# Attention scores of a hybrid decoder step: the two float parts of a query stacked on 128 partitions

## The chip, the cores and the metric

The kernel is one program on one core of a Trainium2 chip. The metric is the device time of one execution in microseconds (us). TensorE is called PE in the rows (its weight loads PEld), VectorE DVE, ScalarE ACT, GpSimd POOL and SyncE SP.

## What is computed

One inference step of one decoder layer, in float32, for 1024 prompt tokens and 64 sample tokens (8 requests of 8) that share the weights:

```python
# per group of tokens
q, k, v, mq, mk, mv, og, ig, lf = project_mixers(rmsnorm(y, g_mix), w_in, ...)   # 1024 -> 2312 columns
att = swa(q, k, v, sinks)            # 8 query heads, 2 key heads of 64; a window of 128 keys
h   = mlstm(mq, mk, mv, ig, lf)      # 4 heads, a matrix memory
y  += concat(att, headnorm(h) * sigmoid(og)) @ w_out
y  += cross_attend(rmsnorm(y), memory keys and values)   # 4 heads of 64, 256 memory tokens
y  += (silu(xn @ w_gate) * (xn @ w_up)) @ w_down         # xn = rmsnorm(y), hidden 2816
out = rmsnorm(y)
```

In the prompt, a block of 128 queries reads its own and the previous block of keys, so one head's scores for one block are a 128 x 256 tile with a contraction over 64. In the cross-attention the scores of one head for one block are 128 x 256 with a contraction over 64 as well. The caches, the states and the memory keys and values are outputs too.

## The kernel before, in words

**Exact float32 by parts.** Every large product is made from fp32r operands. `split` (L101 to L109) rounds an array into a high part on ACT (L102) and puts the remainder, the low part, on DVE (L103, or POOL for some weights). A product is then three matmuls: high x high, high x low, low x high (`mm3`). All matmuls stand under the helper's line L85, so the rows are told apart by their tiles: `mm` is the PSUM tile of the projections, `sc` of the scores, `pt` of transposes, `o` of the attention outputs.

**Order of the stages.** The projections and the mLSTM come first (to about 298 us of the span; the mLSTM's gates use POOL, and its blocks keep `mvx`, `CS` and `QZ` in the slots of tag "c"). Then comes the windowed attention: 16 calls of `swa_unit`, one for a block of 128 queries and a pair of query heads per key head; between the calls a generator, `fill`, hands out projections (the output gate and a part of the output projection) in the numbers of the list `nfill`. Then the output projection of the attention heads and the cross-attention, chunk by chunk of tokens, with eight calls of `cross_unit` between them, and last the FFN, with the final norm and the stores. Engines take their instructions in a fixed order each. A scheduler orders them while the program is built, by the order of the text and by its own estimate of when operands and buffers are ready; so matmuls of different tiles stand interleaved on PE.

**Scores in `swa_unit`.** The query is split into `qhl` (two times 128 columns for the high parts, the same for the low). The two key heads lie on partitions 0 to 63 and 64 to 127, in the keys `khi` and `klo` as in the queries. For each of two query heads the loop runs over the three products and, innermost, over the two key heads: 12 matmuls of 64 rows and 256 columns, whose neighbours use different halves of the rows and write different PSUM banks. DVE then adds the mask and takes the maximum (L703), ACT the exponential (L622), DVE the scaling (L627), PE transposes (L717), ACT copies (L718), and four float32 matmuls on half the columns make the output `o`, which ACT copies into the place of the query (L724).

**Scores in `cross_unit`.** The same with two heads of a feature tile: `qhl` from the projected query `xq`, the memory keys in `kvhl`, 12 matmuls of 64 rows per call, then the maximum (L866, L884), the exponential (L887) and the scaling (L891).

**Buffers.** The slots of tag "c" are nine: in the windowed attention the keys `khi` and `klo`, the values `vp`, the memory's `kvf`, the sample's `VC` and a rotation of `pp`. PSUM has two banks for `sc`, three for `mm`, two for `pt` and one for `o`. Temporary tiles have ten buffers.

Of the kernel before, what the change touches and what calls it, by code (L numbers as in the profile page):

```python
# [9 lines left out]
F32 = mybir.dt.float32  # L10
F32R = mybir.dt.float32r
AF = mybir.ActivationFunctionType
# [3 lines left out]
P = 128  # L16
D = 1024
NK = D // P                 # feature tiles of the model width
TP = 1024                   # prompt tokens
TS = 64                     # sample tokens (8 requests x 8)  # L20
T = TP + TS
NB = TP // P                # prompt token blocks
CH = [(0, 384), (384, 768), (768, 1088)]
CHE = [(0, 416), (416, 832), (832, 1088)]   # where the last one ends the kernel
FT = 22                     # feature tiles of the FFN
# [4 lines left out]
# columns of the vectors packed by the host  # L30
# [3 lines left out]
# columns of the constants  # L34
C_ID, C_ONE, C_CAUS, C_CAUSS, C_BM, C_M0, C_M1 = 0, 128, 256, 384, 448, 456, 712
C_N = 968
# columns of the constants for the gates
# [5 lines left out]
def tile_hymba_step(  # L43
# [79 lines left out]
    def load_ahead(srcs):  # L123
        """The weights in the order of their use, each loaded one step ahead of it."""
        todo, ahead = iter(srcs), []

        def step():
            for src, eng in todo:
                ahead.append(load_w(src, 8, eng=eng))
                break  # L130

        def next_w():
            step()
            return ahead.pop(0)

        step()
        return next_w
# [19 lines left out]
    # ================= stage 1: x, split; sums of squares =================  # L157
# [22 lines left out]
    # the first two tiles run along with the arrival of x  # L180
# [24 lines left out]
    # token-major rstd  # L205
# [150 lines left out]
    # rows (block, head) of prompt; rows (head) of sample  # L356
# [40 lines left out]
    # the weight of the state before the block, as rows  # L397
# [33 lines left out]
    # the upper half of the partitions holds the odd heads  # L431
# [20 lines left out]
    # M4: mq pair 0, mq pair 1, mk pair 0, mk pair 1; later the head outputs  # L452
# [4 lines left out]
    # the heads' norm weights with the half of sigmoid(x) = (1 + tanh(x / 2)) / 2  # L457
# [5 lines left out]
    def mlstm_ps():  # L463
        """PSUM for num | den of the heads: the row tiles of odd and even heads go to different banks."""
        b = [ptps([2, 129]), ptps([2, 129])]
        return b, [b[h % 2][:, h // 2] for h in range(4)]

    def mlstm_w(src, m):
        """The weight of the state, by head pair, on the partitions of the heads."""
        wb = tmp([2, m], name="wb")  # L470
        for h2 in range(2):
            nc.sync.dma_start(wb[h2 * 64:h2 * 64 + 64],
                              src.rearrange("o (j z t) -> o z j t", z=2, t=m)[:, h2].to_broadcast([64, 2, m]))
        return wb

    def mlstm_head_out(nb, blk, m, c0, junk):
        """num | den of the heads in PSUM -> normalised heads, transposed into M4."""
        rec = small(4, "rec", 2)
        for z in range(2):
            V.tensor_copy(rec[:m, z::2], nb[z][:m, :, P])  # L480
        V.scalar_tensor_tensor(rec[:m], rec[:m], -1.0, rec[:m], ALU.mult, ALU.max)
        V.tensor_tensor(rec[:m], rec[:m], emt[:m, blk * 4:blk * 4 + 4], ALU.max)
        V.reciprocal(rec[:m], rec[:m])
        hh = tmp([4, P], name="hh")
        for z in range(2):
            V.tensor_tensor(hh[:m, z::2], nb[z][:m, :, 0:P],
                            rec[:m, z::2].unsqueeze(2).to_broadcast([m, 2, P]), ALU.mult)
        q2 = small(4, "q2", 2)
        for h in range(4):
            A.activation(junk[:m], hh[:m, h, :], AF.Square, accum_out=q2[:m, h:h + 1])  # L490
        done = rstd_from(q2[:m], q2[:m], P)
        V.tensor_tensor(hh[:m], hh[:m], q2[:m].unsqueeze(2).to_broadcast([m, 4, P]), ALU.mult)
        ht = ops([4, P])
        for h in range(4):
            TE.transpose(ht[:, h, :m], hh[:m, h, :], ident[:m, :m])
        for h in range(4):
            A.activation(M4[h][:, c0:c0 + m], ht[:, h, :m], AF.Copy, scale=hg[:, h:h + 1])
        return done

    def mlstm_S(blk, m, c0, bc, caus):  # L500
        """S^T[s, t] of the four heads, weighted."""
        dd = bc
        G.tensor_tensor(dd[:m], caus.unsqueeze(1).to_broadcast([m, 4, m]), bc[:m], ALU.subtract)
        for h in range(4):
            A.activation(dd[:m, h, :], dd[:m, h, :], AF.Exp, bias=gg[:m, blk * 4 + h:blk * 4 + h + 1])
        kq = [scps(), scps()]
        for h in range(4):
            pr = slice((h % 2) * 64, (h % 2) * 64 + 64)
            mm(kq[h % 2][:m, (h // 2) * m:(h // 2) * m + m], M4[2 + h // 2][pr, c0:c0 + m], M4[h // 2][pr, c0:c0 + m])
        S = tmp([4, m], name="S")  # L510
        for h2 in range(2):
            V.tensor_tensor(S[:m, h2::2], kq[h2][:m, 0:2 * m].rearrange("p (j t) -> p j t", j=2),
                            dd[:m, h2::2], ALU.mult)
        return S
# [102 lines left out]
    def softmax_pieces(pieces, mx, nbias, es=None):  # L617
        """P = exp(0.125 s + bias) / (sum + es) in place for the (row, piece) scores."""
        n = len(pieces)
        l = small(4, "l", 2)  # L620
        for i, a in enumerate(pieces):
            A.activation(a, a, AF.Exp, scale=0.125, bias=nbias[:, i:i + 1], accum_out=l[:, i:i + 1])  # L622
        if es is not None:
            V.tensor_tensor(l[:, 0:n], l[:, 0:n], es, ALU.add)
        V.reciprocal(l[:, 0:n], l[:, 0:n])
        for i, a in enumerate(pieces):
            V.tensor_scalar_mul(a, a, l[:, i:i + 1])  # L627
# [56 lines left out]
    def swa_unit(blk, jp):  # L684
        k0 = max(0, (blk - 1) * P)
        mask = c[:, C_M0:C_M0 + 256] if blk == 0 else c[:, C_M1:C_M1 + 256]
        qhl = tmp([2, 2, P], F32R, name="qhl")
        qh, ql = qhl[:, 0], qhl[:, 1]
        for j2 in range(2):
            split(qh[:, j2, :], ql[:, j2, :], qc[2 * jp + j2][:, blk * P:blk * P + P])  # L690
        sc = [scps(), scps()]
        for j2 in range(2):
            cs = slice(j2 * 256, j2 * 256 + 256)
            for z, (a, b_) in enumerate(((qh, khi), (qh, klo), (ql, khi))):
                for kv in range(2):
                    pr = slice(kv * 64, kv * 64 + 64)
                    mm(sc[kv][:, cs], a[pr, j2, :], b_[pr, k0:k0 + 256], z == 0, z == 2)
# [50 lines left out]
    class Next:  # L748
        """Operands of the GEMM behind a norm: (y * g) split; rstd goes on its output."""
# [68 lines left out]
    for u in range(2 * NB):  # L818
        if u == 0:
            swa_sample()  # L820
        swa_unit(u // 2, u % 2)
        for _ in range(nfill[u]):
            next(fill, None)
# [4 lines left out]
    kvhl = slot("c", [4, 256], F32R, name="kvhl")  # L828
    kvh, kvl = kvhl[:, 0:2], kvhl[:, 2:4]
    split(kvh, kvl, kvf[:, 0:2])  # L830
# [5 lines left out]
    # weights of this stage in the order of their use  # L836
# [31 lines left out]
    def cross_unit(pair, f):  # L868
        """Two blocks of prompt tokens, one pair of heads."""
        bs = slice(pair * 256, pair * 256 + 256)  # L870
        qhl = tmp([2, 256], F32R, name="qhl")
        split(qhl[:, 0], qhl[:, 1], xq[f][:, bs])
        sc = [scps(), scps()]
        for i in range(2):
            ts = slice(i * P, i * P + P)
            for z, (a, b_) in enumerate(((0, kvh), (0, kvl), (1, kvh))):
                for h2 in range(2):
                    pr = slice(h2 * 64, h2 * 64 + 64)
                    mm(sc[h2][:, i * 256:i * 256 + 256], qhl[pr, a, ts], b_[pr, f, :], z == 0, z == 2)
# [168 lines left out]
def _consts():  # L1048
# [19 lines left out]
    # sample window: rows (request of the pair, kv, group, token)  # L1068
# [13 lines left out]
def _tiles(w, cols=None):  # L1082
    """[K, F] -> [F/128, 128, K/128, 128]"""
# [5 lines left out]
def _pack(i):  # L1089
# [23 lines left out]
    for base, g in ((V_MIX, a["g_mix"][0]), (V_CROSS, a["g_cross"][0]), (V_FFN, a["g_ffn"][0]),  # L1113
# [5 lines left out]
    s = a["attn_sinks"][0].reshape(2, 2, 2)          # kv, pair, j2  # L1119
# [10 lines left out]
                         a["state_mlstm_n"][0][..., None]], -1)          # b h d 129  # L1130
    r["st_C"] = np.ascontiguousarray(
        st.reshape(4, 2, 4, 64, 129).transpose(1, 3, 0, 2, 4).reshape(P, 4, 4, 129))
    ck = a["cache_mem_k"][0].reshape(8, 256, 2, P)                       # b m f (h2 d)
# [42 lines left out]
```

## Time and profile before

| what | value |
|---|---|
| three runs | 1380.97, 1387.66, 1389.80 us; median 1387.66 |
| profiled execution | span 1380.3 us (first to last instruction; no time of its own is given beside the span) |
| PE, PEld, DVE, ACT, POOL busy | 1343.5, 1266.2, 622.2, 444.6, 190.3 us |
| matmuls | 8352 records, of them 192 scores of the windowed attention and 96 of the cross-attention |
| granted clock of PE | 0.995 of full on average |

A busy share says little by itself: matmuls are pipelined, so that a record of 0.33 us can follow its predecessor after 0.17 us. What one matmul costs is read from the distance between the starts of neighbours. The stages are told apart by time: windowed attention about 298 to 425 us, output projection and cross-attention to about 592 us, FFN from there to the end.

### The profile page before, as it was taken

How to read it: one execution, taken by the hardware profiler on the slowest of the kernel's cores; microseconds unless marked ns; L12 is line 12 of the kernel's file. 1: busy time of each engine (PE TensorE's matmuls, PEld its weight loads, DVE VectorE, ACT ScalarE, POOL GpSimd, SP SyncE). 2: the span in 40 equal slices, each digit the busy share in tenths (PEclk: the TensorE clock that was granted, in tenths of full speed). 3: DMA queues.
4: the chain of work that ended last, by engine and by line, in shares of the span. 5: the costliest groups of instructions: out<-in, count | busy, mean ns of one | idle time of the engine just before them, and what ended most of it. 6: DMA issues, size and time to landing. Idle time of an engine off the chain costs nothing.

```text
span 1380.3 us, 20544 instructions
## 1 busy us (share of the span) xinstructions
PE 1343.5 (97%) x8352; PEld 1266.2 (92%) x8352; DVE 622.2 (45%) x1373; ACT 444.6 (32%) x1024; POOL 190.3 (14%) x167
## 2 busy tenths in 40 slices
PE   7999999999999898999999999999999999999997
PEld 6999988887888786799999999999999999999997
DVE  7224345467766778835323332332233232423245
ACT  4322332447754666721221011201121121112133
POOL 3000110100003551110111011101110011001123
PEclk9999999999999999999999999999999999999999
DMA  5122413110311224102111111111112120111113
GB/s 228 40 74 62 146 56 121 38 47 16 131 46 57 97 92 163 52 16 62 47 31 62 46 47 31 51 42 46 47 32 61 31 62 31 62 32 50 43 37 124
DMA packets 38807, 88.26 MB, mean 64 GB/s; under 512 B 6593, under 2 KB 14209, under 8 KB 38713
## 3 DMA queue, kind: packets, MB, share of 16 engines
q1 hardware_dynamic: 38713, 86.95, 19.6%
q8 instruction: 66, 1.08, 0.3%
q14 instruction: 28, 0.23, 0.1%
HBM read 79.54 MB, written 7.38 MB: 63 GB/s over the span
## 4 chain that ended last, share of the span: by engine, by line
PE 58%; DVE 3%; ACT 1%; issue 0%; DMA 0%; POOL 0%; DVEq 0%; ACTq 0%; POOLq 0%
PE mm L85 57%; DVE nlo L109 1%; PE o L85 0%; DVE y L955 0%; PE pt L85 0%; DVE nb L866 0%; DVE wlo L103 0%; DMA ck<-cm_k 0%; PE sc L85 0%; ACT sp L887 0%; ACT sq L773 0%; DVE qhl L103 0%; DVE ss L777 0%; DVE yo L1043 0%; PE pt L897 0%
## 5 line engine op out<-in xcount | busy, mean ns | idle before, releaser
L85 PE MATMUL mm<-nhi,wlo 128*128 128x384 f32 (+1 forms) x1056 | 344.4, 326 | 0.0
L85 PE MATMUL mm<-nlo,whi 128*128 128x384 f32 (+1 forms) x1056 | 344.1, 326 | 0.0
L85 PE MATMUL mm<-nhi,whi 128*128 128x384 f32 (+1 forms) x1056 | 344.0, 326 | 0.0
L102 ACT ACTIVATE whi<-wraw 128x1024 fp32r<-128x1024 f32 (+1 forms) x105 | 109.4, 1042 | 345.9 <-PE mm L85 295.1
L85 PEld LDWEIGHTS mm<-nhi,whi 128*128 128x128 f32 x1056 | 198.2, 188 | 0.1
L85 PEld LDWEIGHTS mm<-nhi,wlo 128*128 128x128 f32 x1056 | 198.2, 188 | 0.1
L85 PEld LDWEIGHTS mm<-nlo,whi 128*128 128x128 f32 x1056 | 198.2, 188 | 0.0
L1005 POOL TENSOR_TENSOR gate<-gate,rstd 128x384 f32<-128x384 f32 (+1 forms) x66 | 78.3, 1187 | 656.3 <-ACT gate L1004 656.3
L85 PE MATMUL mm<-hlo,whi 128*128 128x384 f32 (+3 forms) x480 | 157.1, 327 | 0.0
L85 PE MATMUL mm<-hhi,whi 128*128 128x384 f32 (+3 forms) x480 | 156.9, 327 | 0.0
L85 PE MATMUL mm<-hhi,wlo 128*128 128x384 f32 (+3 forms) x480 | 156.9, 327 | 0.0
L103 DVE TENSOR_TENSOR wlo<-wraw,whi 128x1024 fp32r<-128x1024 f32 (+1 forms) x93 | 112.1, 1205 | 45.6 <-ACT whi L102 41.9
L1008 DVE TENSOR_TENSOR h<-mm,gate 128x384 f32<-128x384 f32 (+1 forms) x66 | 35.4, 536 | 193.9 <-PE mm L85 189.0
L1018 DVE TENSOR_TENSOR y<-y,mm 128x384 f32<-128x384 f32 (+1 forms) x120 | 63.6, 531 | 118.6 <-PE mm L85 118.6
L85 PE MATMUL mm<-xhi,whi 128*128 128x384 f32 (+1 forms) x288 | 98.6, 342 | 0.0
L85 PE MATMUL mm<-xlo,whi 128*128 128x384 f32 (+1 forms) x288 | 98.1, 341 | 0.0
L85 PE MATMUL mm<-xhi,wlo 128*128 128x384 f32 (+1 forms) x288 | 97.3, 338 | 0.0
L1002 DVE TENSOR_TENSOR gate<-mm,rstd 128x384 f32<-128x384 f32 (+1 forms) x66 | 35.4, 536 | 123.5 <-PE mm L85 123.5
L85 PEld LDWEIGHTS mm<-hlo,whi 128*128 128x128 f32 x480 | 90.1, 188 | 0.4 <-issue 0.3
L85 PEld LDWEIGHTS mm<-hhi,whi 128*128 128x128 f32 x480 | 90.2, 188 | 0.2 <-issue 0.2
L85 PEld LDWEIGHTS mm<-hhi,wlo 128*128 128x128 f32 x480 | 90.2, 188 | 0.2 <-issue 0.2
L102 ACT ACTIVATE hhi<-h 128x384 fp32r<-128x384 f32 (+1 forms) x66 | 33.2, 503 | 158.7 <-DVE h L1008 158.6
(343 smaller groups left out, 2169.6 us busy)
## 6 DMA issues: line engine op xcount, KB each, us to landing
wraw<-wg SPq DMA_DIRECT2D x22, 512.0 KB
wraw<-wu SPq DMA_DIRECT2D x22, 512.0 KB
wraw<-wd SPq DMA_DIRECT2D x40, 256.0 KB
wraw<-wout SPq DMA_DIRECT2D x32, 256.0 KB
wraw<-win_f SPq DMA_DIRECT2D x13, 512.0 KB
xraw<-xT SPq DMA_DIRECT2D x8, 544.0 KB
y<-xT SPq DMA_DIRECT2D x8, 544.0 KB
o_y<-yo SPq DMA_DIRECT2D x16, 208.0 KB
```

Source lines behind the costliest of these rows:

```text
L85: return TE.matmul(out, lhsT, rhs, start=start, stop=stop)
L102: A.activation(hi, src, AF.Copy)
L103: (eng or V).tensor_tensor(lo, src, hi.bitcast(F32), ALU.subtract)
L109: V.scalar_tensor_tensor(lo, src, scale, hi.bitcast(F32), ALU.mult, ALU.subtract)
L1002: V.tensor_tensor(t, ga, fr[:, c0:c1], ALU.mult)
L1005: G.tensor_tensor(t, t, fr[:, c0:c1], ALU.mult)
L1008: V.tensor_tensor(h, ua, t, ALU.mult)
L1018: V.tensor_tensor(y[d][:, c0:c1], y[d][:, c0:c1], acc, ALU.add)
```

## The change: what it does

- The keys of the windowed attention are copied into four new tiles `kst` of the slots "c": for each key head and each part (high, low), the 64 rows stand on both halves of the partitions. POOL makes these eight copies of 64 x 1088.
- A new helper `stack` makes a tile `qst` of a query: for each of the two heads in it, the high part on that head's own half of the partitions and the low part on the other half. That is two ACT and two DVE instructions of 64 x 256 for 256 queries.
- A score is then two matmuls over all 128 rows: (high, low) against the high keys on both halves, and (high, low) against the low keys. The product low x low, left out before, comes in. There are 8 matmuls for a unit instead of 12, and the two key heads come one after the other.
- The units are taken in another order: both blocks of a pair of blocks for one pair of heads, and then the other pair of heads, so that one `stack` serves two units.
- In the cross-attention `kvhl` becomes two tiles `kvs` with the keys of each head on both halves (two splits of 64 x 512 and four POOL copies of 64 x 512), and `cross_unit` uses `stack` and 8 matmuls.

```diff
-    def swa_unit(blk, jp):
+    kst = []
+    for kv in range(2):
+        pr = slice(kv * 64, kv * 64 + 64)
+        both = []
+        for src in (khi, klo):
+            t = slot("c", [T], F32R, name="kst")
+            for z in range(2):
+                G.tensor_copy(t[z * 64:z * 64 + 64], src[pr].bitcast(F32))
+            both.append(t)
+        kst.append(both)
+    def stack(src):
+        st = tmp([2, 256], F32R, name="qst")
+        for z in range(2):
+            p_, q_ = slice(z * 64, z * 64 + 64), slice((1 - z) * 64, (1 - z) * 64 + 64)
+            A.activation(st[p_, z], src[p_], AF.Copy)
+            V.tensor_tensor(st[q_, z], src[p_], st[p_, z].bitcast(F32), ALU.subtract)
+        return st
+    qst = [None, None]
+    def swa_unit(bp, jp, bi):
+        blk = 2 * bp + bi
+        if bi == 0:
+            for j2 in range(2):
+                qst[j2] = stack(qc[2 * jp + j2][:, bp * 256:bp * 256 + 256])
         k0 = max(0, (blk - 1) * P)
         mask = c[:, C_M0:C_M0 + 256] if blk == 0 else c[:, C_M1:C_M1 + 256]
-        qhl = tmp([2, 2, P], F32R, name="qhl")
-        qh, ql = qhl[:, 0], qhl[:, 1]
-        for j2 in range(2):
-            split(qh[:, j2, :], ql[:, j2, :], qc[2 * jp + j2][:, blk * P:blk * P + P])
         sc = [scps(), scps()]
-        for j2 in range(2):
-            cs = slice(j2 * 256, j2 * 256 + 256)
-            for z, (a, b_) in enumerate(((qh, khi), (qh, klo), (ql, khi))):
-                for kv in range(2):
-                    pr = slice(kv * 64, kv * 64 + 64)
-                    mm(sc[kv][:, cs], a[pr, j2, :], b_[pr, k0:k0 + 256], z == 0, z == 2)
+        for kv in range(2):
+            for j2 in range(2):
+                cs = slice(j2 * 256, j2 * 256 + 256)
+                for z in range(2):
+                    mm(sc[kv][:, cs], qst[j2][:, kv, bi * P:bi * P + P], kst[kv][z][:, k0:k0 + 256],
+                       z == 0, z == 1)
 ...
-        swa_unit(u // 2, u % 2)
+        swa_unit(u // 4, u // 2 % 2, u % 2)
 ...
-    kvhl = slot("c", [4, 256], F32R, name="kvhl")
-    kvh, kvl = kvhl[:, 0:2], kvhl[:, 2:4]
-    split(kvh, kvl, kvf[:, 0:2])
+    kvs = [slot("c", [2, 2, 256], F32R, name="kvs") for _ in range(2)]
+    for h2 in range(2):
+        pr, po = slice(h2 * 64, h2 * 64 + 64), slice((1 - h2) * 64, (1 - h2) * 64 + 64)
+        split(kvs[0][pr, h2], kvs[1][pr, h2], kvf[pr, 0:2])
+        for z in range(2):
+            G.tensor_copy(kvs[z][po, h2], kvs[z][pr, h2].bitcast(F32))
 ...
     def cross_unit(pair, f):
-        """Two blocks of prompt tokens, one pair of heads."""
         bs = slice(pair * 256, pair * 256 + 256)
-        qhl = tmp([2, 256], F32R, name="qhl")
-        split(qhl[:, 0], qhl[:, 1], xq[f][:, bs])
+        st = stack(xq[f][:, bs])
         sc = [scps(), scps()]
-        for i in range(2):
-            ts = slice(i * P, i * P + P)
-            for z, (a, b_) in enumerate(((0, kvh), (0, kvl), (1, kvh))):
-                for h2 in range(2):
-                    pr = slice(h2 * 64, h2 * 64 + 64)
-                    mm(sc[h2][:, i * 256:i * 256 + 256], qhl[pr, a, ts], b_[pr, f, :], z == 0, z == 2)
+        for h2 in range(2):
+            for i in range(2):
+                for z in range(2):
+                    mm(sc[h2][:, i * 256:i * 256 + 256], st[:, h2, i * P:i * P + P], kvs[z][:, h2, f, :],
+                       z == 0, z == 1)
```

The rest of the diff removes comments.

## Rows read from the trace of the kernel before

**Rows 1.** The page's head and part 1: busy us (share) and instructions by engine.

```profile
span 1380.3 us, 20544 instructions
...
PE 1343.5 (97%) x8352; PEld 1266.2 (92%) x8352; DVE 622.2 (45%) x1373; ACT 444.6 (32%) x1024; POOL 190.3 (14%) x167
```

**Rows 2.** Stretches: length; PE, PEld, DVE, ACT, POOL busy us (instructions); clock; DMA.

```profile
298.00:355.00 57.00, 56.83 (x377) 43.32 (x376) 38.16 (x177) 38.02 (x136) 0.00 (x0) 0.94 0.06 20
355.00:425.00 70.00, 67.56 (x465) 56.87 (x464) 50.51 (x174) 43.55 (x137) 2.50 (x1) 1.00 0.28 95
465.00:535.00 70.00, 64.20 (x433) 55.11 (x434) 53.96 (x110) 45.42 (x112) 29.32 (x20) 1.00 0.36 118
535.00:575.00 40.00, 35.25 (x229) 25.43 (x229) 34.83 (x84) 25.88 (x68) 6.42 (x6) 0.96 0.31 97
```

**Rows 3.** The chain that ended last: start us, length us, what.

```profile
591.32 746.82 PE mm L85 x4522
```

**Rows 4.** PE's timeline, a unit's scores in one run: start us, length us, what.

```profile
402.47 0.39 PE L85 MATMUL sc<-khi,qhl 64*128 64x256 f32 x2
402.70 0.28 PE L85 MATMUL sc<-klo,qhl 64*128 64x256 f32 x2
...
403.38 0.44 PE L85 MATMUL mm<-chi,whi 128*128 128x384 f32 x1
403.66 0.34 PE L85 MATMUL mm<-clo,whi 128*128 128x384 f32 x1
```

**Rows 5.** PE's timeline, two scores between projections.

```profile
321.63 0.34 PE L85 MATMUL mm<-xhi,whi 128*128 128x384 f32 x1
321.90 0.38 PE L85 MATMUL sc<-khi,qhl 64*128 64x256 f32 x1
322.12 0.28 PE L85 MATMUL sc<-klo,qhl 64*128 64x256 f32 x1
322.33 0.44 PE L85 MATMUL mm<-xlo,whi 128*128 128x384 f32 x1
322.61 0.34 PE L85 MATMUL mm<-xhi,wlo 128*128 128x384 f32 x1
```

**Rows 6.** A stretch, instructions of `sc` alone: length; PE, PEld, DVE, ACT busy.

```profile
304.60:355.00 50.40, 13.32 (x106) 8.88 (x104) 11.96 (x32) 0.00 (x0) 1.00 0.07 22
```

**Rows 7.** Waits from 290 to 425 us: total us, times, longest.

```profile
PEld sc L85 <- issue: 6.2, 22, 0.4
```

**Rows 8.** PE's timeline, matmuls of 128 rows and 256 columns in the FFN.

```profile
1362.02 0.28 PE L85 MATMUL mm<-hhi,whi 128*128 128x256 f32 x1
1362.14 0.28 PE L85 MATMUL mm<-hlo,whi 128*128 128x256 f32 x1
```

**Rows 9.** Instructions of `qhl`: duration ns min/median/max, first and last start.

```profile
L102 ACT ACTIVATE qhl<-qc x32: 292/308/313, 290.1 to 403.2; 128x128 fp32r<-128x128 f32 x32
L103 DVE TENSOR_TENSOR qhl<-qc,qhl x32: 260/285/293, 292.7 to 405.1; 128x128 fp32r<-128x128 f32 x32
L102 ACT ACTIVATE qhl<-xq x8: 399/417/435, 464.7 to 561.8; 128x256 fp32r<-128x256 f32 x8
L103 DVE TENSOR_TENSOR qhl<-xq,qhl x8: 421/426/1479, 465.1 to 563.4; 128x256 fp32r<-128x256 f32 x8
```

**Rows 10.** Groups on POOL, by form: busy us, mean ns, idle before.

```profile
L178 POOL TENSOR_TENSOR sq<-sq 128x1088 f32<-128x1088 f32 x3 | 9.8, 3268 | 10.1 <-ACT sq L174 9.9
...
L537 POOL MEMSET QZ<- 128x1088 f32 x1 | 1.0, 1006 | 11.2 <-PE o L85 11.2
```

**Rows 11.** Timeline around a POOL instruction at 418 us.

```profile
418.33 2.50 POOL L103 TENSOR_TENSOR wlo<-wraw,whi 128x1024 fp32r<-128x1024 f32 x1 [150.65 <-ACT whi L102]
418.55 2.44 DVE L627 TENSOR_SCALAR sp<-sp,l 128x256 f32<-128x256 f32 x1
...
421.04 0.44 PE L717 MATMUL pt<-c,sp 128*128 128x128 f32 x2 [1.91 <-DVE sp L627]
```

**Rows 12.** Group of the scaling of the weights on DVE, by form.

```profile
L627 DVE TENSOR_SCALAR sp<-sp,l 128x256 f32<-128x256 f32 x64 | 20.3, 382 | 0.3
```

## The prediction

> **What bounds the kernel now.** I read the page first: PE is busy for 1343.5 of 1380.3 us [rows 1]. Then the chain that ended last: from 591 us it is one piece of 747 us of matmuls [rows 3]. What is won or lost before 591 us therefore reaches the end whole. Then the view by stretches [rows 2]. In the windowed attention PE is busy for 56.8 of 57 and 67.6 of 70 us, while DVE and ACT stay at 61 to 72%: PE is the bound there. In the cross-attention PE is busy for 64.2 of 70 us from 465 and for 35.3 of 40 us from 535, where DVE has 34.8: there PE waits and DVE is near its limit. So a PE saving counts in the first stage, and DVE work counts in the second.
>
> Last I read PE's timeline for what a score costs, by distances between starts. In one long run of twelve, matmuls on the two halves of the rows start in pairs, two records at one time [rows 4]. The run takes 403.38 - 402.47 = 0.91 us, or 0.076 us a matmul. The first projection behind it takes 0.28 us until its successor starts, where 0.17 us is usual: 0.11 us more. A score placed between projections is much dearer [rows 5]. The projection at 321.63 would be through at 321.80; two scores follow; the projection at 322.33 starts its successor at 322.61, so that without delay it would have begun at 322.44. Two scores thus took 0.64 us. Had they been one more pair in a long run, they would have taken about 0.12. So an interruption costs a fixed 0.4 to 0.5 us, for whose delay the waits view names no instruction: 22 waits of a score's weight load, 6.2 us, released by "issue" [rows 7].
>
> **The change part by part.**
>
> *Fewer passes, but wider ones.* A matmul of 128 rows and 256 columns starts 0.12 us behind the last one [rows 8]. A unit's scores become 8 x 0.12 = 0.96 us, all in the mode of the projections and transposes. Against a long run, at 0.91 + 0.11 = 1.02 us, 0.06 is won; but the runs of rows 4 stand behind `o`, which works on half the columns, and that change of mode stays, now paid by the first score (about 0.11). So such a unit loses about 0.05 us. Six of the 16 windowed units and about six of the eight cross units stand so: +0.6 us.
>
> The row shows paired starts. The Trainium skill (TensorEngine Tiling (Array Packing), Theoretical Speedup) says that two tiles of 64 rows give up to twice the speed, which speaks against this change. By that rule alone a unit goes from 6 passes to 8, and 24 units cost 24 x 2 x 0.12 = 5.8 us more. The trace agrees within a run and not at its ends, and the ends are what I think decides; the page itself adds (Key Properties) that a change of mode drains the array.
>
> *Interruptions.* Between 304.6 and 355 us the scores keep PE busy for 13.3 us with 106 matmuls [rows 6], 0.126 us each against 0.076 in a long run. I count 22 runs of scores in PE's timeline of that stretch. Before: 13.3 + 22 x 0.11 for the projection behind each = 15.7 us. After: 106 x 8/12 = 71 matmuls at 0.12 = 8.5 us, and 1.0 us for about ten sides of runs that border on `o` and keep their change of mode. That would be -6.2 us. The order on PE may differ, but a score in any place then costs 0.12.
>
> *Splitting the query.* In the windowed attention `stack` needs as many instructions as `split` did, 32 on ACT and 32 on DVE, each twice as wide and on half the partitions. The price of 256 columns stands on `xq`: 417 ns on ACT and 426 on DVE, against 308 and 285 for 128 [rows 9]. I take half the partitions to cost the same. That is ACT +3.5 and DVE +4.5 us in a stage where both have 28 to 39% free [rows 2]: nothing, hidden by PE; without that cover up to 4.5 us. The first score of every second unit waits for a chain about 0.8 us longer, hidden by the projections that PE has beside it.
>
> In the cross-attention the instructions double: 8 more on each, ACT +3.3 and DVE +3.4 us. The two units behind 535 us meet a nearly full DVE: 0.85 us in full. The other six add 2.6 us on DVE where PE already waits for 5.8 of 70 us; I take half. Together +2.1 us, between 0 and 3.4. Behind a longer DVE queue stand the residual additions and norm operands, and PE's projections wait for these.
>
> *The key copies on POOL.* The trace has no copy on POOL. Bounds for 1088 columns: 1.0 us (a memset) and 3.3 us (a sum of two tensors) [rows 10]; one tensor is read, so I take 2. Eight are 8 to 26 us. They need only `khi`, `klo` and four slots "c", which come free as the mLSTM's tiles die, and `VC` now gets its slot after them. POOL has only the mLSTM's short instructions then, and PE has the projections of q and of the gate. The first windowed score runs at 298 us; I cost them at nothing. The four copies for `kvs` (512 columns, 0.5 to 1.5 us each by the same rows) should come when the last scores have freed `kst`, ahead of or beside the weights that POOL splits from 418 us on: nothing too, at most 6 us if these wait. `pp` has two or three slots instead of about five, enough for a tile that lives for one unit. The extra split of the memory keys, about 0.7 us on ACT and DVE, falls beside the last projections of the fill.
>
> **The sum.** +0.6 - 6.2 + 2.1 = -3.5 us on the profiled 1380.3: 1376.8. The profiled span is the low end of the three runs, whose median is 1387.66; the prediction is for the median, 1387.7 - 3.5 = 1384 us.
>
> **Rivals.**
>
> *A. No gain: passes against passes.* The interruptions may be waits for operands, which the rows call "issue" because nothing is recorded; then they stay, and the wider scores add their passes. For it: the fragments are at their thickest where the query is split late. Against it: two scores in rows 5 whose neighbours had no recorded wait. By the pass count: 71 x 0.12 = 8.5 us against 106 x 0.076 = 8.1 us, plus the cross-attention's 2.1 and the long runs' 0.6: +3.1, 1391 us. By the skill's rule taken alone it would be +5.8 + 2.1, 1396 us.
>
> *B. Slower: POOL's copies hold up DVE.* At 418 us one POOL instruction of 2.50 us stretched a DVE scaling to 2.44 us [rows 11] from the usual 0.38 [rows 12], and PE's transposes waited 1.91 us for it. The change adds twelve POOL instructions. If each costs PE what that one did, 12 x 1.9 = 23 us come on top: 1384 + 23 = 1407 us; if only the four of `kvs` do, 1392. It decides when the copies fall where PE has no projection ready to run; the eight of `kst` fall where it has, and only `kvs` near a place like 418 us. The Trainium skill (SBUF — State Buffer, two separate sides) calls the port pair of DVE and POOL an exclusive lock held for a whole instruction; the row at 418 us agrees.
>
> *C. More gain.* DVE's additions hide in the cross-attention (-2.1), and the new order loses the half-clock stretch at the first unit (granted clock 0.94 over 298 to 355 [rows 2], so about 57 x 0.06 = 3.4 us): 1384 - 5.5 = 1378.5; with the POOL stall at 418 us gone as well, 1376.5.
>
> *D. It doesn't do what it says.* If the scheduler's order made the first windowed scores wait for the last key copy, PE would run projections first and meet the attention's own chain, uncovered, behind them. I count this within B: its price is the same order, and the same copies decide.
>
> **How the numbers follow.** My forecast 0.50, A 0.20, B 0.17, C 0.13. A measurement of this kernel can tell about 1%, 14 us, from no change: the bounds are 1374 and 1401.5 us. The forecast, A and most of C lie within. Faster by over 1% needs C in full and a little more: 0.11. Slower by over 1% needs most of B: 0.13. The rest is 0.76. The range reaches from C with a further 4 us, since the scheduler's order may move stalls of about that size, to the middle of B: 1373 to 1397 us.
>
> **What would show it.** Right: records of scores on 128 rows start 0.12 us apart, and a projection behind them takes 0.17 us; PE's busy time falls by about 6 us between 298 and 425 us and the FFN starts some 3 us sooner, with the same length. The waits of the scores' weight loads for "issue" are gone. DVE in the cross-attention is up by 3 us, with PE's waits there up by about 2. Wrong: scores that still stand with gaps around them (A); long DVE instructions beside POOL copies with PE idle (B); a first windowed score later than 298 us (D). The prediction falls altogether if the order of the whole attention stage changes its length by more than these terms, or if a copy on POOL to other partitions costs far more than 3.3 us.

## The result and the profile after

The changed kernel takes 1397.89 us (median of 5 runs, 1393.51 to 1403.67); the kernel before, beside it, 1384.94 (5 runs, 1380.97 to 1389.80). The ratio is 1.008, interval [1.0052, 1.0109]: slower by 7 to 15 us. The forecast was 1384 and a gain of 3.5; the range ended at 1397. The profiled execution of before was one of its fastest (span 1380.3), that of after an ordinary one (1396.4), so some of the 16.1 us between the two traces is luck: 4.7 us of it lie ahead of the first changed instruction. POOL's memset of `QZ` starts at 210.25 us for 205.54, and from 160 us up to there the granted clock is 0.93, where the kernel before has 1.00. The trace of `e2_cross_only` below, whose code up to there is before's, has 0.94 there.

The head of the page and its first part, as in [rows 1]:

```profile
span 1396.4 us, 20373 instructions
...
PE 1350.3 (97%) x8256; PEld 1276.4 (91%) x8256; DVE 639.7 (46%) x1382; ACT 455.5 (33%) x1033; POOL 201.2 (14%) x179
```

There are 96 matmuls fewer, as the change says, and yet PE is busy 6.8 us longer: a matmul's record grows where the clock is halved, and the granted clock is 0.988 on average over this trace and 0.995 over that of before. DVE, ACT and POOL have 17.5, 10.9 and 10.9 us more.

Where the time went is read by stages, with bounds set by events and not by the clock on the wall: from the first product of the sample's block (`QZ`) to the mLSTM's last norm; from the first windowed score to its last output; from the first `xq` to the FFN's first `h`. Columns as in [rows 2]. The kernel before:

```profile
214.00:282.40 68.40, 67.72 (x446) 57.07 (x446) 33.66 (x100) 23.34 (x86) 8.99 (x13) 1.00 0.26 83
298.00:423.20 125.20, 122.59 (x829) 98.39 (x828) 88.14 (x351) 81.12 (x269) 2.50 (x1) 0.97 0.18 61
464.10:595.30 131.20, 120.37 (x781) 99.35 (x780) 103.09 (x223) 86.52 (x210) 39.67 (x30) 0.99 0.29 93
```

The changed kernel, the same stages:

```profile
218.70:293.10 74.40, 71.99 (x446) 60.34 (x445) 35.75 (x100) 23.29 (x86) 18.62 (x21) 0.95 0.24 76
310.10:432.10 122.00, 118.50 (x759) 98.32 (x758) 94.17 (x349) 87.09 (x269) 3.54 (x2) 0.98 0.18 63
473.90:610.80 136.90, 120.84 (x745) 101.38 (x744) 109.49 (x231) 91.01 (x218) 39.05 (x30) 0.98 0.28 89
```

The windowed attention is 3.2 us shorter, with PE busy 4.1 us less: that is the gain looked for. About 1.4 us of it, an estimate, is where the half-clock stretch at the first unit falls: 6.5 us of it lie inside this window before (298.0 to 304.5) and 3.6 inside it now (310.1 to 313.7), and half of the difference is lost time. The mLSTM, which the change doesn't touch, is 6.0 us longer at the same count of matmuls, with POOL's eight copies in it (13 instructions become 21) and a granted clock of 0.95 for 1.00. The cross-attention is 5.7 us longer with PE's busy time unchanged: PE is idle for 16.1 us there instead of 10.8. The FFN is as long as before (785.6 us, and 785.0 in the kernel before), so every loss reaches the end, as [rows 3] said.

The scores themselves, by starts. A whole unit behind `o` and a projection, as in [rows 4]:

```profile
410.77 0.44 PE L85 MATMUL mm<-chi,wlo 128*128 128x384 f32 x1
411.06 1.11 PE L85 MATMUL sc<-kst,qst 128*128 128x256 f32 x8
412.00 0.34 PE L85 MATMUL mm<-chi,whi 128*128 128x384 f32 x1
412.18 0.34 PE L85 MATMUL mm<-clo,whi 128*128 128x384 f32 x1
```

Half a unit between projections, as in [rows 5]:

```profile
338.48 0.31 PE L85 MATMUL mm<-xlo,whi 128*128 128x320 f32 x1
338.63 0.71 PE L85 MATMUL sc<-kst,qst 128*128 128x256 f32 x4
339.18 0.31 PE L85 MATMUL mm<-xhi,wlo 128*128 128x320 f32 x1
339.32 0.31 PE L85 MATMUL mm<-xhi,whi 128*128 128x320 f32 x1
```

Eight take 0.94 us, 0.118 each, and the projection behind them 0.18. Four between projections take 0.55, 0.138 each, with no gap ahead and none behind, where two took 0.64 before. Busy time hides this: a stretch of the length of [rows 6], behind the half-clock one, has

```profile
314.00:364.40 50.40, 12.66 (x72) 9.97 (x72) 13.00 (x35) 0.00 (x0) 1.00 0.07 22
```

12.7 us for 72 scores, hardly less than 13.3 for 106, because the last record of each run (0.28 us) reaches 0.14 us into the projection that has begun behind it; the starts have to be read. What is left of the waits of [rows 7], from 300 to 432 us:

```profile
PEld sc L85 <- issue: 3.1, 8, 0.4
```

There are 8 for 22. In PE's order a run of scores stands directly behind `o`, which still works on half the columns, eight times (before as well), so these are the ones that had to stay. The instructions of `qst`, as in [rows 9]:

```profile
L701 ACT ACTIVATE qst<-qc x32: 402/414/419, 300.8 to 403.4; 64x256 fp32r<-64x256 f32 x32
L702 DVE TENSOR_TENSOR qst<-qc,qst x32: 418/420/424, 303.4 to 406.1; 64x256 fp32r<-64x256 f32 x32
L701 ACT ACTIVATE qst<-xq x16: 400/413/418, 474.4 to 575.9; 64x256 fp32r<-64x256 f32 x16
L702 DVE TENSOR_TENSOR qst<-xq,qst x16: 418/420/423, 475.0 to 577.9; 64x256 fp32r<-64x256 f32 x16
```

Half the partitions cost what all of them did, as assumed. The key copies lie at the lower of the two bounds from [rows 10]:

```profile
L692 POOL CAST kst<-khi x4: 1088/1092/1092, 223.6 to 249.7; 64x1088 fp32r<-64x1088 f32 x4
L692 POOL CAST kst<-klo x4: 1082/1094/1976, 244.4 to 252.0; 64x1088 fp32r<-64x1088 f32 x4
```

1.09 us each (one of the eight 1.98), and 0.61 for the cross-attention's (one of the four 1.06). They start at 223.6 us, amid the sample's block of the mLSTM, and there the projections that PE has at hand run out before what follows is ready. The longest wait of PE for DVE in that stretch, after POOL's first two copies:

```profile
227.80 1.55 PE L85 MATMUL sc<-mvs,kz 64*128 64x129 f32 x8 [1.66 <-DVE kz L562]
```

The same product in the kernel before, without a wait:

```profile
221.37 1.16 PE L85 MATMUL sc<-mvs,kz 64*128 64x129 f32 x8
```

The stall of [rows 11] is still there, 8 us later in the span; it neither went nor multiplied:

```profile
426.22 2.48 POOL L103 TENSOR_TENSOR wlo<-wraw,whi 128x1024 fp32r<-128x1024 f32 x1 [148.63 <-ACT whi L102]
...
428.91 0.44 PE L740 MATMUL pt<-c,sp 128*128 128x128 f32 x2 [1.91 <-DVE sp L627]
```

### The profile page after: what moved, and what is told of

Read it like the earlier page. It is cut to its first block, busy times and chain, and to the rows that moved or that the text cites. A ratio compares the mean times of both kernels' runs of the same rounds, so it can differ in the third digit from the quotient of the medians.

```text
span 1396.4 us, 20373 instructions
## 1 busy us (share of the span) xinstructions
PE 1350.3 (97%) x8256; PEld 1276.4 (91%) x8256; DVE 639.7 (46%) x1382; ACT 455.5 (33%) x1033; POOL 201.2 (14%) x179
## 3 DMA queue, kind: packets, MB, share of 16 engines
q8 instruction: 65, 1.06, 0.3%
## 4 chain that ended last, share of the span: by engine, by line
PE 85%; DVE 8%; ACT 4%; issue 1%; DMA 1%; POOL 0%; SPq 0%; DVEq 0%; ACTq 0%; POOLq 0%
PE mm L85 75%; PE sc L85 3%; PE o L85 3%; PE pt L85 2%; PE pt L740 1%; DVE nhl L109 1%; DVE nb L892 1%; DVE wlo L103 1%; DVE nb L908 1%; PE pt L921 1%; DVE qst L702 0%; DVE sp L627 0%; ACT whi L102 0%; DMA wraw<-win_f 0%; DVE nlo L109 0%
```

## The experiments

All ratios are against the kernel before in the same set of runs, with a 95% interval; 0.1% is 1.4 us.

### First set: which part loses

- `e1_swa_only`: the windowed attention as changed, with its copies; the cross-attention's code as before.
- `e2_cross_only`: the reverse.
- `e3_copies_only`: the windowed scores as before, three passes of 64 rows, but reading the copied tiles: `mm(sc[kv][:, cs], a[pr, j2, :], kst[kv][p][pr, k0:k0 + 256], ...)`.
- `e4_no_copies`: the stacked scores without any copy, over `khi` and `klo` as they lie, so that a head's low parts meet the other head's keys:

```diff
-                    mm(..., qst[j2][:, kv, bi * P:bi * P + P], kst[kv][z][:, k0:k0 + 256], z == 0, z == 1)
+                    mm(..., qst[j2][:, kv, bi * P:bi * P + P], (khi, klo)[z][:, k0:k0 + 256], z == 0, z == 1)
```

> The windowed attention changed, the cross-attention as before. Theory 1 (POOL's key copies hold up DVE in the mLSTM stage and cost 7 to 9 us, the cross-attention's part of the change costs 5, the windowed scores themselves win 3): 1385 + 8 - 3 = about 1390 us. Theory 2 (the mLSTM stage only looked slower in that one profile, the loss is the cross-attention's): 1385 - 3 = about 1382 us. Theory 3 (the wider scores lose): 1395 us or more.

> The cross-attention changed, the windowed attention as before. Theory 1: 1385 + 5 = about 1390 us, with the FFN reached some 5 us later and the stages before 425 us unchanged. Theory 2: 1385 + 13 = about 1398 us. Theory 3: 1385 to 1388 us.

> The eight key copies are made, and the scores are those of before (twelve matmuls of 64 rows, units in the order of before), reading the half of the copy that belongs to the head. Theory 1: 1385 + 7 to 9 = 1392 to 1394 us, with DVE instructions of the sample's mLSTM block stretched beside the copies. Theory 2: 1385 us. Theory 3: 1385 us.

> The stacked scores without the copies: the eight matmuls read the keys of before over all 128 rows, so that a head's low part meets the other head's keys and the scores are not the reference's. Cross-attention as before. Theory 1: 1385 - 3 = about 1382 us, and the windowed attention 3 us shorter than before. Theory 2: 1382 us too. Theory 3: 1395 us.

Measured: e1 1.0056 [1.0036, 1.0076]; e2 1.0052 [1.0035, 1.0069]; e3 1.0065 [1.0042, 1.0088]; e4 0.9984 [0.9971, 0.9996]. So the stacked scores win 2.2 us, the key copies alone lose 9, and the cross-attention loses 7: 14 in sum, inside the 7 to 15 of the whole. The theories that put all of it on one part, or on the wider scores, fall.

In e3's trace the loss is seen where it arises. From the memset of `QZ` (205.5 us in both) to the first copy, its starts agree with those of before within 0.1 us. POOL, and DVE beside it:

```profile
218.88 2.23 POOL L692 CAST kst<-khi 64x1088 fp32r<-64x1088 f32 x2 [11.69 <-PE pt L85]
...
238.36 3.12 POOL L692 CAST kst<-klo 64x1088 fp32r<-64x1088 f32 x2 [15.91 <-DMA o_Cs<-CS]
241.54 1.09 POOL L692 CAST kst<-khi 64x1088 fp32r<-64x1088 f32 x1
242.71 0.88 POOL L586 TENSOR_TENSOR wb<-mqk,wb 128x128 f32<-128x128 f32 x2
```

```profile
218.79 0.15 DVE L480 COPY rec<-pt 64x2 f32<-64x2 f32 x1 [1.23 <-PE pt L85]
218.97 1.01 DVE L481 SCALAR_TENSOR_TENSOR rec<-rec 64x4 f32<-64x4 f32 x1
220.01 1.09 DVE L482 TENSOR_TENSOR rec<-rec,g_em 64x4 f32<-64x4 f32 x1
```

The same in the kernel before:

```profile
219.03 0.15 DVE L481 SCALAR_TENSOR_TENSOR rec<-rec 64x4 f32<-64x4 f32 x1
219.22 0.15 DVE L482 TENSOR_TENSOR rec<-rec,g_em 64x4 f32<-64x4 f32 x1
...
237.84 0.88 POOL L586 TENSOR_TENSOR wb<-mqk,wb 128x128 f32<-128x128 f32 x2 [8.92 <-DMA wb<-Wd]
```

Two things are late. DVE's instructions on four columns end when POOL's two copies end, 1.01 and 1.09 us for 0.15. This agrees with what the Trainium skill (SBUF — State Buffer, two separate sides) says of a lock that POOL or DVE holds for a whole instruction. And `wb`, the weighted queries of the next block, waits in POOL's own queue behind three copies: 242.71 for 237.84. The trace of the kernel before already had such a long DVE instruction, beside a POOL product:

```profile
241.62 1.29 POOL L503 TENSOR_TENSOR bc<-c,bc 128x512 f32<-128x512 f32 x1 [2.90 <-PE pt L85]
241.85 1.07 DVE L481 SCALAR_TENSOR_TENSOR rec<-rec 128x4 f32<-128x4 f32 x1
```

What PE loses by it in e3: `kz`, which DVE makes behind these short instructions, comes late, and PE's projections run out 1.66 us before it. From there to the next products with `kz` the granted clock is 0.73 (columns as in [rows 2]), where the kernel before has 1.00:

```profile
223.04 1.16 PE L85 MATMUL sc<-mvs,kz 64*128 64x129 f32 x8 [1.66 <-DVE kz L562]
```

```profile
223.04:229.36 6.32, 6.32 (x33) 5.35 (x33) 4.06 (x10) 2.89 (x13) 0.00 (x0) 0.73 0.01 3
```

The mLSTM ends at 287.1 us in e3 and at 282.4 before, 4.7 us later. The wait is 1.66 of that and the clock about 1.7, an estimate (6.32 x 0.27); the rest isn't traced. For `wb` the waits view has no wait of PE, so what its delay cost is not shown. The wait of 1.65 to 1.66 us for `kz` stands in all three traces with POOL's copies in this place (e1, e3, the changed kernel), each time with half the clock within 3 us behind it; no other trace of the case has it.

### Second set: the copy, or the tile; the cross-attention's parts

`w_late` keeps POOL's copies but moves them behind the memset of `QB`, the last of POOL's work for the sample's attention, and takes their tiles later too; `w_dma` keeps the place and takes the work from POOL:

```diff
-                G.tensor_copy(t[z * 64:z * 64 + 64], src[pr].bitcast(F32))
+                nc.sync.dma_start(t[z * 64:z * 64 + 64].bitcast(F32), src[pr].bitcast(F32))
```

`x_kvs` and `x_nocopy` take the cross-attention apart (windowed code as before): the one has the copied keys with `split` and 64-row passes, the other `stack` and 128-row passes over `kvhl`.

> Windowed stage as changed, cross-attention as before. The four key tiles and POOL's eight casts are the same, but they are taken behind the sample's loads, and the casts stand in POOL's queue behind the memset of QB (267 us in the profile of before) and not amid the sample's mLSTM (224 to 253 us in the changed kernel). Theory K (what costs is that the casts and their tiles lie amid the sample's block: DVE's short instructions beside them take 1.0 us for 0.15, and the order around it changes): most of the 9 us comes back, 1382 to 1385 us. Rival L (eight casts cost wherever they lie, because DVE's later head outputs and the output gate are held in the same way, or the scores start late): 1388 to 1392 us.

> Windowed stage as changed, cross-attention as before; the eight key copies are DMAs on SP's queue (64x1088 each), and POOL has none. The four tiles are taken where the changed kernel takes them. Theory K1 (POOL's casts hold DVE up): 1382 to 1385 us, as without copies. Rival K2 (the tiles taken early push back the load of VC, from 218.9 to 253.1 us in the changed kernel's profile, and reorder DVE and SP around the sample's block; who copies doesn't matter): 1389 to 1393 us, or more where the eight DMAs hold up the weights queued behind them on SP.

> Windowed stage as before. In the cross-attention only the keys are changed: the two tiles with four POOL copies of 64x512, while the queries are split as before and the scores are before's passes of 64 rows, read from each head's own half. Theory C1 (the cross-attention loses by DVE's second subtraction for each unit and what it pushes back): 1384 to 1386 us, nothing lost. Rival C2 (it loses by the key copies and the two half-width splits ahead of them): 1389 to 1393 us.

> Windowed stage as before. In the cross-attention the queries' two parts stand over one another and the scores are two passes of 128 rows, but the keys are before's split over 128 rows with no copies (so each head's lower rows meet the other head's keys: other values, the same work for PE). Theory C1: 1389 to 1393 us, all of the cross-attention's loss. Rival C2: 1382 to 1385 us. Both by halves: 1387 to 1389 us for this one and for the one with the key copies alone.

Measured: w_late 0.9974 [0.9954, 0.9995]; w_dma 0.9964 [0.9941, 0.9986]; x_kvs 1.0005 [0.9983, 1.0027]; x_nocopy 1.0037 [1.0013, 1.0062]. K2 and L fall: with the same tiles, taken at the same place, 9 us are back when POOL doesn't copy, and with the same POOL copies they are back when these stand behind the block. `w_dma`'s trace has the short instructions short again, and POOL's `wb` with no copy ahead of it (this execution is 1.5 us later from `QZ` on):

```profile
220.54 0.15 DVE L481 SCALAR_TENSOR_TENSOR rec<-rec 64x4 f32<-64x4 f32 x1
220.73 0.15 DVE L482 TENSOR_TENSOR rec<-rec,g_em 64x4 f32<-64x4 f32 x1
```

```profile
239.61 0.88 POOL L586 TENSOR_TENSOR wb<-mqk,wb 128x128 f32<-128x128 f32 x2 [11.71 <-DMA wb<-Wd]
```

Both versions beat both kernels, the kernel before by 3.6 and 5.0 us. In the cross-attention C1 holds: the keys cost nothing, the queries and scores do.

### Third set: the doubled split or the wider passes; a last placement

`x_onesplit`: 128-row passes over before's `split` of the query. `x_q`: `stack` and the copied keys, with before's 64-row passes. `w_latedma`: DMAs, and the tiles taken behind the sample's loads.

> Windowed stage as before. In the cross-attention the scores are two passes of 128 rows as in the change, but the queries are split as before (one cast and one subtraction over 128 rows for a unit) and the keys are before's, without copies; so the two halves hold the two heads' parts and the values are others, with the same work for PE. Theory C1 (the loss is the doubled split of the queries): 1380 to 1384 us, the stacked scores' small gain and no loss. Rival C3 (the loss comes with the stacked passes themselves, which change what PE does between the units and so when DVE and POOL meet): 1388 to 1392 us, as with the doubled split.

> Windowed stage as before. In the cross-attention the keys and the doubled split of the queries are as changed, and the scores are before's three passes of 64 rows over them (the third pass of each head reads the other head's low part: other values, the same work). Theory C1: 1390 to 1394 us, all of the loss or a little more. Rival C3: 1384 to 1387 us.

> The version that the runs so far point to: stacked scores in the windowed attention alone, the key copies as DMAs on SP's queue and taken behind the sample's loads, the cross-attention as before. Theory K1 with the stacked scores' gain: 1380 to 1383 us, a ratio of 0.996 to 0.998. Rival (the eight DMAs, now later in the queue, hold up the loads of bc and of the weights behind them): 1384 to 1390 us.

Measured: x_onesplit 1.001 [0.999, 1.0029]; x_q 1.0047 [1.0028, 1.0065]; w_latedma 1.0005 [0.9979, 1.003]. The doubled split loses with either kind of pass and the wide passes without it don't lose: C1. But they don't win here either, where 1380 to 1384 was expected. From the first `xq` to the first `h` x_onesplit's trace has 130.9 us, before 131.2: the units are through sooner (108.3 us for 111.9) and leave projections standing behind them (22.6 us for 19.3).

`w_latedma` missed. In its trace SP's queue has the last block's `wb` behind two weight loads of the output projection, which wait for a buffer: it is issued at 285.9 us, where before had it at 261.6, and POOL's product with it starts at 289.6, where before had it at 266.3. From `QZ`'s memset its mLSTM takes 83.6 us, and 78.0 in `w_dma`. A queue that was not the bound became it.

### Fourth and fifth set: why 0.4 us in a unit costs so much

Eight more instructions on each of DVE and ACT, 0.42 us each, cost 5 to 7 us (x_nocopy, x_q, e2). `b_dve` and `b_act` add one of them to the kernel before, ahead of the scores; `b_acto` and `b_dveo` add the same length behind the unit (a part of the output copied onto itself):

```diff
+        A.activation(qhl[:, 0], xq[f][:, bs], AF.Copy)                                      # b_act
         split(qhl[:, 0], qhl[:, 1], xq[f][:, bs])
+        V.tensor_tensor(qhl[:, 1], xq[f][:, bs], qhl[:, 0].bitcast(F32), ALU.subtract)      # b_dve
...
         split(oc[f][0][:, bs], oc[f][1][:, bs], o)
+        A.activation(oc[f][0][:, bs], oc[f][0][:, bs].bitcast(F32), AF.Copy)                # b_acto
...
+        V.tensor_copy(oc[f][1][:, bs], oc[f][1][:, bs].bitcast(F32))                        # b_dveo
```

`x_relief` is e2 with half of the scaling (L891 in before) on ACT. `after_dma` is the whole change with the eight copies of the windowed keys as DMAs.

> The kernel before, with one thing added: in each of the cross-attention's eight units DVE makes the low part of the queries a second time (128x256, about 0.42 us). Theory C1a (the doubled split costs through DVE, whose queue in the cross-attention leaves the fewest gaps): 1388 to 1392 us, most of the doubled split's loss. Theory C1b (it costs through ACT and the longer chain ahead of the scores): 1384 to 1387 us.

> The kernel before, with one thing added: in each of the cross-attention's eight units ACT casts the queries' high part a second time (128x256, about 0.42 us), ahead of the subtraction. C1a: 1384 to 1387 us. C1b: 1388 to 1392 us.

> The cross-attention as changed and the windowed stage as before, but the scaling of the second head's probabilities (16 of 32 instructions of 0.43 us on DVE) is done by ACT. C1a: DVE has 7 us less and the loss is gone or better, 1380 to 1386 us. C1b: ACT has 6 to 7 us more in the same stage, 1391 us or more.

> The changed kernel with the eight key copies of the windowed stage as DMAs on SP's queue, all else as changed (POOL's four small copies of the cross-attention's keys too). If the two losses add up, what is left is the stacked scores' gain of 2 to 5 us and the doubled split's loss of 5 to 7: 1386 to 1390 us. If the losses are not separate (one delay, seen twice): 1380 to 1384 us, or unchanged at 1396.

> The kernel before, with one thing added: behind each of the cross-attention's eight units ACT copies the finished high part of the outputs onto itself (128x256, about 0.4 us). It stands behind the unit, not between the queries and their scores. Theory D1 (0.4 us costs more than its length only on the chain from the queries to the scores): 1384 to 1386 us. Rival D2 (an instruction of 0.4 us on ACT costs as much wherever it stands in the unit): 1389 to 1394 us, as with the second cast of the queries.

> The same with DVE: behind each unit it copies the finished low part of the outputs onto itself (128x256). D1: 1384 to 1386 us. D2: 1388 to 1392 us, as with the second subtraction.

Measured: b_dve 1.0048 [1.0026, 1.0071]; b_act 1.0063 [1.0043, 1.0084]; x_relief 1.0034 [1.0012, 1.0056]; after_dma 1.0055 [1.003, 1.0079]; b_acto 1.0001 [0.9981, 1.0021]; b_dveo 1.0005 [0.9983, 1.0027].

Neither C1a nor C1b as put: the engine doesn't matter, the place does. 8 x 0.42 = 3.4 us ahead of the scores cost 6.6 and 8.7 us; behind the unit they cost nothing that is measured, on either engine. Taking 7 us from DVE (`x_relief`) brought back less than 3 of 7, not clear of its interval. PE's busy time and waits in the stage, in `b_act` and in `b_acto`, columns as in [rows 2]; both have eight ACT instructions more than before (218 for 210):

```profile
467.60:605.50 137.90, 123.44 (x777) 98.56 (x776) 105.20 (x224) 89.83 (x218) 40.00 (x30) 0.99 0.27 89
```

```profile
465.70:594.30 128.60, 117.87 (x777) 97.43 (x776) 104.03 (x224) 89.32 (x218) 39.86 (x30) 1.00 0.29 95
```

PE is idle for 14.5 us in the first and for 10.7 in the second, as in the kernel before (10.8). Its waits in `b_act`:

```profile
PE pt L898 <- DVE sp L892: 6.5, 8, 2.1
PE sc L85 <- DVE qhl L103: 3.4, 3, 1.6
PE mm L85 <- DVE y L956: 3.2, 4, 1.3
PE sc L85 <- ACT qhl L102: 1.1, 2, 0.7
```

and in the changed kernel, from 473.9 to 610.8 us:

```profile
PE pt L921 <- DVE sp L915: 6.9, 6, 1.9
PE mm L85 <- DVE y L979: 4.7, 4, 3.1
PE sc L85 <- DVE qst L702: 1.4, 3, 0.8
```

In the kernel before the first two are 4.2 and 2.6 us, and in `b_acto` 5.3 and 2.2. I read this so: scores that come late make the softmax and the transposes late, and PE, which takes its instructions in order, stands before them with projections behind. The waits are only a part of it: in `b_act` the stage is 6.7 us longer than before, 3.6 of them idle time of PE and 3.1 busy time. Part may lie in the order of PE: the scheduler wrote another for each of these kernels, and it was not held fixed. So the place is shown, and the path from there to PE is argued.

`after_dma` is 1.0055 and the whole change 1.008, in different sets: the DMAs bring back 3.5 us between the two ratios, where they bring back 13 without the new cross-attention (e1 against w_dma). The intervals allow anything from nothing to 9, so that the two losses add up is not shown, only that neither is the other. Its mLSTM takes the 78.0 us from `QZ`'s memset that `w_dma`'s takes (the changed kernel 82.9, before 76.9), and the wait for `kz` is gone.

## Why the prediction was wrong

- **Wider scores without a change of mode:** right. 0.118 us each was forecast as 0.12, and the fragments' extra cost is gone where they stand between projections (0.138 each).
- **Interruptions, -6.2 us (with the clean units -5.6):** right in mechanism, too large. The stage is 3.2 us shorter, PE busy there 4.1 less; without copies the gain is 2.2 us [0.6, 4.0] by e4, with copies out of POOL's way 3.6 and 5.0 by w_late and w_dma. The step priced a score between projections at 0.12; the starts show 0.138, which is 1.3 us on 71. PE's other waits in the stage grew from 2.6 to 3.5 us, and the runs behind `o` kept their change of mode, as was allowed for.
- **"POOL has only the mLSTM's short instructions then, and PE has the projections": the step that failed.** The copies' own length was overestimated (2 us for 1.09) and still they cost 9 us [5.8, 12.2], where 0 was put. The cover named did not last: in the sample's block a product of PE needs DVE's chain, the copies held that chain up by 1.7 us, and PE ran out of projections for 1.66 us (e3), with half the clock behind it. Rival B had the mechanism and excluded these eight of its twelve copies; the four that it feared cost 0.7 us [-2.4, 3.7] (x_kvs). The extra tiles and the later load of `VC` cost nothing (w_dma).
- **The cross-attention, +2.1 us, between 0 and 3.4: mis-sized.** It costs 7.2 [4.8, 9.6] (e2). The step added the instructions' busy time on DVE, in full or by half. It left out that they stand ahead of the scores: there the added 0.42 us cost about twice its length on DVE (b_dve) and 2.6 times on ACT (b_act), behind the unit nothing that is measured (b_acto, b_dveo).
- **The sum.** -2.2 + 9.0 + 7.2 = 14.0 by the parts; the whole is 7 to 15. The forecast's -3.5 had two terms too small, by 9 and by 5 us, and one gain too large by 1 to 3.
- **A sign that misled.** The first windowed score starts at 310.1 us for 298, which was to show rival D. It doesn't: POOL's last key copy starts at 252.0 us, long before, and 4.7 us of the delay lie ahead of any changed code.
- **The clock.** The prediction's terms hold no clock, except in rival C, whose half-clock stretch at the first unit stayed. e3's mLSTM is 4.7 us longer in its trace and the kernel 9 by its runs. The granted clock, averaged over the runs, is 0.990 in e3 and 0.994 in the kernel before beside it, and in e1 0.987. What that is worth is read from the kernel before alone: its executions at 0.990 span 1387.6 us on average, those at 0.996 1380.7, so 1.1 us for 0.001. By that estimate some 4 of e3's 9 us and nearly all of e1's 8 are lost clock; in e2 it is 2 of 7. With the copies out of POOL's way it is as before (w_late 0.993, w_dma 0.994, before 0.993). That a copy lowers the clock is still not shown: `x_kvs`, `x_q` and `x_relief`, whose code up to there is before's, have a half-clock stretch between 230 and 248 us without that wait, and after_dma, without POOL's windowed copies, has 0.990 over its runs, beside 0.994 before.

## What to carry to other kernels

Where a step is hidden "because the engine is free", look at what the engine's neighbours do in exactly those microseconds: a copy of 1 us on POOL is not free beside a chain of 0.15 us instructions on DVE; a DMA, or a place behind that chain, was here (w_dma, w_late), while DMAs in another place of SP's queue gave the gain away again (w_latedma). And price an added instruction by its place: on the chain that feeds PE it can cost twice its length, behind it nothing.

## What the runs showed of the hardware

A POOL copy of 64 x 1088, to the same half of the partitions or to the other, takes 1.09 us, hardly more than the memset of 1088 columns at 1.00 and a third of the sum at 3.27 [rows 10]. Beside it a DVE instruction on four columns lasts as long as the copy, seven times its own 0.15 us.
